# The third pair of the last step of both MLPs takes seven products

## The chip, the cores and the metric

One core of a Trainium2 chip runs the whole program. The metric is the time of one execution on the device, in microseconds. TensorE (PE) multiplies, VectorE (DVE) and ScalarE (ACT) work on elements, GpSimd (POOL) and SyncE (SP) mostly issue transfers here.

## The reference

A decoder trunk of two layers on 256 tokens of width 2048, everything float32. Every sub-layer is `h = h + rmsnorm(f(rmsnorm(h)))`. Layer 0 is a gated convolution and an MLP; then a shared K and V are projected; layer 1 is an attention without softmax and another MLP. The MLP has a hidden width of 8192:

```python
def sq_relu_mlp(u, w_up, w_down):
    return jnp.square(jax.nn.relu(u @ w_up)) @ w_down
```

The change concerns only the down product of the two MLPs, and of it one piece of 256 hidden units by 1024 output columns.

## The kernel before, in words

**Precision.** Each operand of a product is split into a rounded high part and the rest, the low part. A product of two blocks is three matmuls into the same PSUM bank: high by high, high by low, low by high (L1194 to L1196 in `products`, L327 to L329 in `Group.half`). The high parts of weights are written by ScalarE (L174), the low parts by VectorE (L185).

**Weights.** The weights are one stream of chunks of 128 x 1024, in the order in which they are used. SP loads a chunk into one of five `raw` buffers (`load_one`, L158). `split_one` rounds it into one of seven ring buffers `hi` and one of seven `lo`. A raw buffer takes the next load when its chunk is split; a ring buffer is free when PE has used its chunk. `chunk(i)` asks for splits up to four chunks ahead.

**The MLP.** It goes in 8 steps of 1024 hidden units (8 hidden tiles of 128, 4 pairs). In step e, PE alternates between one hidden tile of step e+1 (`whole_up`) and one pair of step e on the way down (`Down.pair`). Down goes by two halves of 1024 columns. The last step has no tile to make any more: in its first half the four pairs follow each other on PE (`for m in range(4): down.pair(...)`), and the second half is a plain `Group` of eight chunks on the banks 6, 7, 0 and 1 (`LAST_BANKS`). In the first MLP its last four chunks are taken block by block (`KeyNorms`, edge 4), in the second its last six (`OutNorms`, edge 6): there the chunks 762 to 767 all go by the first block and the first 512 columns before anything else, so they follow each other within 0.68 us each.

**Eight products or seven.** A pair is two hidden tiles by two token blocks, times two chunks of two column halves of 512: a 2 x 2 block product. `Down.eight` does it plainly with 8 products into four banks. `Down.seven` does it with 7 products, from sums of the blocks (Winograd's form of Strassen's algorithm). It needs sums of the weights, made by `split_seven` (four subtractions of 128 x 512, L211, then seven half-chunks to round and to subtract instead of four, in four ring buffers a, b, t, u instead of two), and sums of the hidden blocks, made by `Hidden.sums_of` (four of 128 x 128, L1056, and their splits, L1012 and L1013). Four of its products, with the keys 1, 5, 6 and 7, are collected over several pairs in banks 6, 7, 0 and 1. They are added crosswise to the results afterwards: during the steps through memory by POOL's transfers (`add_later`), in the last step at once by VectorE (`add_now`: one copy on ScalarE, L1165, and eight adds on VectorE, L1166 to L1172).

**Which pairs take seven.** The table `SEVEN` holds, for each step and half, the pairs with seven products. In the steps 0 to 6 all pairs take seven. In the last step, before the change, only pair 0 of the first half does. A pair with seven in one half alone is `apart`: its hidden tiles are also split plainly, and its first sum gets a tile of its own with the tag "d".

**When the shared products end.** `Down.range` gives the pair at which each bank's collecting begins and ends. The banks of the keys 1, 5, 6 and 7 end at the last pair with seven products; there `add_now` is put into the program. The second half takes these four banks next.

**What sets the order.** PE's order is that of the program. For VectorE and ScalarE a planner lists the instructions by their place in the program and by when it reckons them ready, `tc.high_priority()` ahead of others; each engine then takes its list in order. The sums of the last pair into the results (L1141), their squares (ScalarE) and gains (L503) are of high priority. From the last chunks of the second half on (`begin`), VectorE and ScalarE too follow the program.

Of the kernel before, what the change touches and what calls it, by code (L numbers as in the profile page):

```python
# [10 lines left out]
F32R = mybir.dt.float32r  # L11
# [3 lines left out]
P = 128  # L15
# [31 lines left out]
STEPS = 8  # L47
# [2 lines left out]
DOWN_BANKS = {(0, 0): 3, (0, 1): 4, (1, 0): 5, (1, 1): UP_BANK, 1: 6, 5: 7, 6: 0, 7: 1}  # L50
LAST_BANKS = [[6, 7], [0, 1]]
OUT_SEVENS = (4, 6)
SEVEN = [((0, 1, 2, 3),) * 2] * (STEPS - 1) + [((0,), ())]
ORDER = ((0, 1, 2, 3), (1, 2, 3, 0))

IN_N = [j * KD + i for i in range(KD) for j in range(3)]
# [40 lines left out]
def trunk(ctx, tc, x, xT, vecs, rows, ws, out):  # L97
# [906 lines left out]
    def mlp(pool, i, before, after):  # L1004
# [5 lines left out]
        def two_parts(parts, src):  # L1010
            hi, lo = parts
            nc.scalar.activation(hi, src, AF.Copy)  # L1012
            nc.vector.tensor_tensor(lo, src, hi.bitcast(F32), op=ALU.subtract)  # L1013

        class Hidden:


            def __init__(self, e):
                self.xs, self.sums = [None] * (NF // 4), {}
                first, second = SEVEN[e]  # L1020
                self.pairs = [2 * m for m in first]
# [23 lines left out]
            def sums_of(self, n, both):  # L1045

                t = after.dump()
                s2, s3, s4 = (t[:, j * P : (j + 1) * P] for j in range(3))
                a11, a21, a12, a22 = (both[:, j // 2, j % 2 * P : (j % 2 + 1) * P] for j in range(4))
                apart = n in self.apart  # L1050
                s1 = t[:, 3 * P :] if apart else a21
                for to, v, w, op in (
                    (s3, a11, a21, ALU.subtract), (s1, a21, a22, ALU.add),
                    (s2, s1, a11, ALU.subtract), (s4, a12, s2, ALU.subtract),
                ):
                    nc.vector.tensor_tensor(to, v, w, op=op)  # L1056
                if apart:
                    one = pool.tile([P, 2, P], F32R, tag="d", name="sums", bufs=1)
                    one = [one[:, j, :] for j in range(2)]
                    two_parts(one, s1)  # L1060
                else:
                    one = self.x(n, 1)
                    hi, lo = (self.xs[n // 4][:, n % 4 : n % 4 + 2, j] for j in range(2))
                    two_parts((hi, lo), both[:].rearrange("p k (b t) -> p k b t", b=NB))
                more = pool.tile([P, 6 * P], F32R, tag="hg", name="sums", bufs=5)
                more = [more[:, j * 3 * P : (j + 1) * 3 * P] for j in range(2)]
                two_parts(more, t[:, : 3 * P])
                return [one] + [[m[:, j * P : (j + 1) * P] for m in more] for j in range(3)]
# [105 lines left out]
        class Down:  # L1174


            def __init__(self, j, plan):
                self.j, self.plan, self.ps = j, plan, {}
                sevens_at = [at for at in plan if at[1] in SEVEN[at[0]][at[2]]]
                whole_at = [at for at in plan if at not in sevens_at and at[0] == STEPS - 1]  # L1180
# [17 lines left out]
            def pair(self, at, first, xs):  # L1198
                e, m, _ = at
                seven = m in SEVEN[e][at[2]]  # L1200
                (self.seven if seven else self.eight)(at, first, xs, 2 * m)
# [34 lines left out]
        for e in range(STEPS):  # L1236
            for h in range(2):
                for m in SEVEN[e][h]:
                    n = 16 * h + 4 * ORDER[h].index(m) + 2 if e < STEPS - 1 else 8 * h + 2 * m
# [308 lines left out]
```

## Time and profile before

| | us |
|---|---|
| median of 3 runs | 2097.27 (2096.62 to 2098.21) |
| the profiled execution | 2096.79 |
| its span on the core | 2095.0 |
| TensorE busy | 2079.7 (99%) |
| VectorE busy | 1888.3 (90%) |
| ScalarE busy | 1456.1 (70%) |

One execution was profiled; its page gives shares of the span, and the trace gives each instruction's start and duration in microseconds from the start of the span. The duration of a matmul's row covers its way through the array, and the next one starts before it ends. A row such as `DVE L185 TENSOR_TENSOR wlo<-raw,whi` is an operation of VectorE at line 185 that writes a low part; what stands in brackets is how long the engine was idle before it and what ended that. Chunks with sums carry their number and letter (`whi752a`); plain chunks have none in these rows and are counted.

### The profile page before, as it was taken

The numbers are of one execution on the slowest core, as the hardware profiler recorded it, in microseconds if no ns is written. First come the engines' busy times: TensorE is split into PE (matmuls) and PEld (weight loads), VectorE is DVE, ScalarE is ACT, GpSimd is POOL, SyncE is SP. The second block draws the span as 40 slices with busy tenths as digits, with TensorE's granted clock in tenths as the row PEclk, the third lists the DMA queues.
The fourth block names the chain that finished last, engine by engine and source line by source line (L and its number), as shares of the span: only waits on it lengthen the run. The fifth ranks groups of instructions, "written<-read, shape, count | busy, mean of one in ns | idle before, by whom it ended". The sixth has DMA issues, their size and how long they took to land.

```text
span 2095.0 us, 29733 instructions
## 1 busy us (share of the span) xinstructions
PE 2079.7 (99%) x10566; PEld 1774.8 (85%) x10566; DVE 1888.3 (90%) x2811; ACT 1456.1 (70%) x2132; POOL 112.6 (5%) x137
## 2 busy tenths in 40 slices
PE   9999999999999999999999999999999999999998
PEld 8888888888888888888888888889888888888886
DVE  8999996999999999999766777658999999999997
ACT  8666554776777777777567888547877767677773
POOL 0000000000100101001000000000001010010010
PEclk9999999999999999999999999999999999999999
DMA  8467674677778878779575555665687787787884
GB/s 291 149 204 251 199 248 155 193 231 227 239 221 234 237 217 251 224 230 261 181 220 167 161 161 161 221 181 171 181 256 232 221 241 225 233 245 219 232 241 164
DMA packets 132341, 449.23 MB, mean 214 GB/s; under 512 B 14816, under 2 KB 15072, under 8 KB 131168
## 3 DMA queue, kind: packets, MB, share of 16 engines
q1 hardware_dynamic: 113184, 406.55, 60.9%
q0 software_dynamic: 18720, 40.38, 9.7%
q8 instruction: 83, 1.36, 0.3%
q14 instruction: 66, 0.54, 0.1%
q10 hardware_dynamic: 288, 0.39, 0.1%
HBM read 413.19 MB, written 2.10 MB: 198 GB/s over the span
## 4 chain that ended last, share of the span: by engine, by line
PE 94%; DVE 4%; issue 1%; DMA 1%; ACT 0%; SPq 0%; DVEq 0%; ACTq 0%
PE up L1081 21%; PE up L1088 12%; PE acc L327 7%; PE acc L329 7%; PE acc L328 7%; PE more L1195 5%; PE more L1194 5%; PE more L1196 5%; PE acc L813 5%; PE acc L1194 4%; PE acc L1195 4%; PE acc L1196 4%; DVE wlo L185 1%; PE up L1083 1%; PE tr L264 1%
## 5 line engine op out<-in xcount | busy, mean ns | idle before, releaser
L185 DVE TENSOR_TENSOR wlo<-raw,whi 128x1024 fp32r<-128x1024 f32 (+1 forms) x414 | 495.9, 1207 | 67.6 <-ACT whi L174 67.3
L174 ACT ACTIVATE whi<-raw 128x1024 fp32r<-128x1024 f32 (+1 forms) x414 | 424.7, 1044 | 152.3 <-PE acc L329 63.5
L1081 PE MATMUL up<-u,whi 128*128 128x512 f32 x1952 | 465.0, 389 | 0.0
L1081 PEld LDWEIGHTS up<-u,whi 128*128 128x128 f32 x1952 | 365.0, 188 | 74.7
L1088 PEld LDWEIGHTS up<-u,wlo 128*128 128x128 f32 x2048 | 263.6, 191 | 10.3
L1088 PE MATMUL up<-u,wlo 128*128 128x256 f32 x2048 | 268.1, 283 | 0.0
L211 DVE TENSOR_TENSOR sums<-raw,sums 128x512 f32<-128x512 f32 x260 | 179.3, 690 | 0.9
L187 DVE SCALAR_TENSOR_TENSOR wlo<-raw,gv,whi 128x512 fp32r<-128x512 f32 (+1 forms) x160 | 131.9, 854 | 41.7 <-ACT whi L174 40.9
L174 ACT ACTIVATE whi<-raw,gv 128x512 fp32r<-128x512 f32 (+1 forms) x160 | 121.6, 800 | 48.6 <-PE acc L329 42.2
L327 PE MATMUL acc<-whi,u 128*128 128x512 f32 x384 | 153.1, 399 | 0.1
L329 PE MATMUL acc<-whi,u 128*128 128x512 f32 x384 | 149.9, 390 | 0.0
L328 PE MATMUL acc<-wlo,u 128*128 128x512 f32 x384 | 149.8, 390 | 0.0
L1094 ACT ACTIVATE half<-up 128x256 f32<-128x256 f32 x128 | 49.1, 385 | 129.8 <-PE up L1088 127.2
L1101 POOL DMA_DIRECT2D mg<-more x108 | 94.0, 870 | 825.8 <-ACT more L1156 423.9
L813 PE MATMUL acc<-u,whi 128*128 128x512 f32 x416 | 98.9, 391 | 2.7 <-DVE sum L822 2.7
L211 DVE TENSOR_TENSOR sums<-raw,raw 128x512 f32<-128x512 f32 x130 | 89.8, 691 | 7.2 <-DMA raw<-w_mlp 7.1
L813 PEld LDWEIGHTS acc<-u,whi 128*128 128x128 f32 x416 | 77.4, 188 | 20.5 <-DVE sum L822 3.7
L211 DVE TENSOR_TENSOR sums<-raw 128x512 f32<-128x512 f32 x130 | 89.8, 691 | 2.2 <-DMA raw<-w_mlp 1.6
L329 PEld LDWEIGHTS acc<-whi,u 128*128 128x128 f32 x384 | 72.1, 188 | 15.4
L327 PEld LDWEIGHTS acc<-whi,u 128*128 128x128 f32 x384 | 72.2, 188 | 13.9 <-ACT tk L1380 0.6
L328 PEld LDWEIGHTS acc<-wlo,u 128*128 128x128 f32 x384 | 72.3, 188 | 13.4
L1034 ACT ACTIVATE s<-s 128x256 f32<-128x256 f32 x128 | 52.1, 411 | 12.1 <-DVE s L1033 11.6
(6686 smaller groups left out, 4589.3 us busy)
## 6 DMA issues: line engine op xcount, KB each, us to landing
raw<-w_mlp SPq DMA_DIRECT2D x512, 512.0 KB, 4.6
raw<-w_in SPq DMA_DIRECT2D x94, 512.0 KB, 4.5
mg<-more POOLq DMA_DIRECT2D x108, 256.0 KB, 6.2
raw<-w_out SPq DMA_DIRECT2D x32, 512.0 KB, 4.6
raw<-w_v SPq DMA_DIRECT2D x32, 512.0 KB, 4.5
raw<-w_k SPq DMA_DIRECT2D x32, 512.0 KB, 4.4
raw<-w_q SPq DMA_DIRECT2D x32, 512.0 KB, 4.3
raw<-w_wo SPq DMA_DIRECT2D x32, 512.0 KB, 3.8
```

The lines of the kernel that those rows point to most:

```text
L174: rounded = nc.scalar.activation(hi[:, at], raw[i][:, at], AF.Copy, scale=1.0 if gain is None else gain)
L185: nc.vector.tensor_tensor(lo[:, at], t[:, at], hi[:, at].bitcast(F32), op=ALU.subtract)
L211: nc.vector.tensor_tensor(t, x, y, op=ALU.subtract)
L327: nc.tensor.matmul(ps[:], xh, hi[:, a], start=i == 0 and k == 0, stop=False)
L328: nc.tensor.matmul(ps[:], xh, lo[:, a], start=False, stop=False)
L329: nc.tensor.matmul(ps[:], xl, hi[:, a], start=False, stop=i == self.n - 1 and k == self.ks - 1)
L813: nc.tensor.matmul(ps[:, :cols], w, xs[:, :cols], start=k == 0 and part == parts[0], stop=k == KD - 1 and part == parts[1], skip_group_che ...
L1081: nc.tensor.matmul(ps, weight(0, first, m), x, start=k == 0, stop=False)
L1088: nc.tensor.matmul(pss[n][:, :T], weight(1, first, m), x, start=False, stop=k == KD - 1)
L1194: nc.tensor.matmul(self.ps[key][:], xh, hi, start=first, stop=False)
L1195: nc.tensor.matmul(self.ps[key][:], xh, lo, start=False, stop=False)
L1196: self.done = nc.tensor.matmul(self.ps[key][:], xl, hi, start=False, stop=last)
```

## The change

The third pair (number 2) of the last step is added to the pairs with seven products, in the first half of the columns, in both MLPs. The tag "d" gets a second buffer, since now two pairs of that step are `apart`.

```diff
-SEVEN = [((0, 1, 2, 3),) * 2] * (STEPS - 1) + [((0,), ())]
+SEVEN = [((0, 1, 2, 3),) * 2] * (STEPS - 1) + [((0, 2), ())]
...
                 if apart:
-                    one = pool.tile([P, 2, P], F32R, tag="d", name="sums", bufs=1)
+                    one = pool.tile([P, 2, P], F32R, tag="d", name="sums", bufs=2)
```

What follows from the table: pair 2 goes through `Down.seven`, its two chunks through `split_seven`, its hidden tiles through `sums_of` as well. The keys 1, 5, 6 and 7 are collected until pair 2, so `add_now` comes behind pair 2 rather than behind pair 0, with one pair left before the second half takes their banks. The bank of the eight-product pairs' last block collects pairs 1 and 3 only.

## The prediction

> **What bounds the kernel now.** I read the page first (engine shares, clock, chain that ended last), then the stretches of the last step of the second MLP, then the timelines of TensorE, VectorE and ScalarE there, and the same of the first MLP. First the page:
>
> ```profile
> PE 2079.7 (99%) x10566; PEld 1774.8 (85%) x10566; DVE 1888.3 (90%) x2811; ACT 1456.1 (70%) x2132; POOL 112.6 (5%) x137
> PEclk9999999999999999999999999999999999999999
> PE 94%; DVE 4%; issue 1%; DMA 1%; ACT 0%; SPq 0%; DVEq 0%; ACTq 0%
> ```
>
> TensorE carries 94% of the chain at full clock, so products taken away are time, as long as what feeds them is ready. VectorE, at 90%, is second. The table by stretch cuts the second MLP's last step at its pairs (columns: stretch, its length, then PE, PEld, DVE, ACT, POOL busy with counts, clock, DMA share, GB/s):
>
> ```profile
> 2043.50:2048.30 4.80, 4.80 (x23) 3.96 (x22) 4.80 (x6) 3.66 (x5) 0.87 (x1) 1.00 0.89 218
> 2048.30:2053.70 5.40, 5.40 (x25) 4.49 (x24) 5.40 (x9) 2.59 (x3) 0.55 (x1) 1.00 1.04 376
> 2053.70:2059.20 5.50, 5.50 (x26) 4.54 (x25) 4.07 (x4) 2.07 (x3) 0.00 (x0) 1.00 0.97 357
> 2059.20:2064.60 5.40, 5.40 (x25) 4.47 (x24) 4.82 (x6) 2.74 (x5) 0.00 (x0) 1.00 0.57 222
> 2064.60:2070.00 5.40, 5.40 (x25) 4.50 (x24) 5.20 (x6) 4.69 (x9) 0.00 (x0) 1.00 0.01 2
> ```
>
> Here PE never rests, VectorE is full for 10 us and nearly full later, and ScalarE has room everywhere. So the question is what VectorE's new work does to weight parts that PE will want.
>
> **What goes: products.** Pair starts on PE (start, duration, line, operands):
>
> ```profile
> 2043.52 0.39 PE L1194 MATMUL more<-whi752a,hid 128*128 128x512 f32 x1
> 2048.28 0.39 PE L1194 MATMUL acc<-whi,hid 128*128 128x512 f32 x1
> 2053.72 0.39 PE L1194 MATMUL acc<-whi,hid 128*128 128x512 f32 x1
> 2064.60 0.39 PE L327 MATMUL acc<-whi,hid 128*128 128x512 f32 x1
> 2073.44 0.39 PE L327 MATMUL acc<-whi,hid 128*128 128x512 f32 x1
> ```
>
> Chunks are counted as in the trace's names: the second MLP's last step begins at 752, so the third pair is 756/757, the fourth 758/759, the eight chunks of the second half 760 to 767. The seven-product pair (21 matmuls) takes 2048.28 - 2043.52 = 4.76 us, the eight-product pair (24) 5.44 us; a matmul costs 0.227 us of issue, not the 0.39 of its row, since they overlap. The change takes 3 x 0.227 = **0.68 us** off PE in each MLP, 1.36 in all, and no more: this is the ceiling of the gain.
>
> **What comes: VectorE and ScalarE work.** The first pair's split shows what the third will cost:
>
> ```profile
> 2034.61 0.69 DVE L211 TENSOR_TENSOR sums<-raw 128x512 f32<-128x512 f32 x1
> ...
> 2036.41 0.69 DVE L185 TENSOR_TENSOR wlo752a<-raw,whi752a 128x512 fp32r<-128x512 f32 x1
> 2037.01 0.69 DVE L211 TENSOR_TENSOR sums<-raw,sums 128x512 f32<-128x512 f32 x1
> 2038.04 1.23 DVE L185 TENSOR_TENSOR wlo752b<-raw,whi752b 128x1024 fp32r<-128x1024 f32 x1 [0.34 <-PE up L1088]
> 2039.19 1.22 DVE L185 TENSOR_TENSOR wlo752t<-sums,whi752t 128x1024 fp32r<-128x1024 f32 x1
> ...
> 2042.18 2.51 DVE L185 TENSOR_TENSOR wlo<-raw,whi 128x1024 fp32r<-128x1024 f32 x2 [0.23 <-ACT whi L174]
> 2044.60 0.42 DVE L259 TENSOR_TENSOR hid<-s,hid 128x256 fp32r<-128x256 f32 x1
> 2044.94 1.22 DVE L185 TENSOR_TENSOR wlo<-raw,whi 128x1024 fp32r<-128x1024 f32 x1
> ```
>
> From start to start a 128x512 costs 0.60 us and a 128x1024 1.13. The split of the third pair becomes 4 sums (2.40) + low part a (0.60) + b, t, u (3.39) = 6.39 us in place of 2 x 1.13 = 2.26: **+4.13 us**. The sums of the hidden pair are made once more; the first pair's are these:
>
> ```profile
> 1981.52 0.29 DVE L1056 TENSOR_TENSOR sq<-s 128x128 f32<-128x128 f32 x1
> 1983.40 0.29 DVE L1013 TENSOR_TENSOR sums<-sq,sums 128x128 fp32r<-128x128 f32 x1
> 1985.54 0.56 DVE L1013 TENSOR_TENSOR sums<-sq,sums 128x384 fp32r<-128x384 f32 x1
> ...
> 2024.43 0.42 DVE L259 TENSOR_TENSOR hid<-s,hid 128x256 fp32r<-128x256 f32 x1
> ```
>
> Four small sums and the small split at 0.20 from start to start, the wide split 0.47: **+1.47 us**, from about 2024 on, since the third pair's second hidden tile is split at 2024.43 (the last row). ScalarE gets 3 half-width roundings more (about 0.48 each) and two small ones, some 2 us; its stretches above leave 1 to 3 us free in each, so this I cost at nothing. The second buffer of tag "d" costs no instruction; it only lets the second set of sums exist beside the first. The hg buffers: five, and a sixth set is wanted in step 7, but step 6 is through with its pair 1 three pairs before its end at 2043.52, before 2024: nothing.
>
> **The Trainium skill on this price.** VectorE: DVE Perf Modes, section "The DRAIN you can't avoid", says that the next VectorE operation doesn't start until the pipe is empty. By it operations stand behind each other at their full 0.69 and 1.22 us, the split grows by 4.67 us, the list of 17.15 us reckoned below by about an eighth, and the sum comes to some +2.3 us. The rows start 0.60 and 1.13 apart, so the trace disagrees and its spacing is used.
>
> **What moves: the adding of the shared products.** Keys 1, 5, 6, 7 now end with the third pair, not the first, so add_now (one ScalarE copy, eight VectorE adds, no DMA) runs about 10 us later. Before, and behind it:
>
> ```profile
> 2046.07 0.69 DVE L1172 TENSOR_TENSOR mg<-mg,more 128x512 f32<-128x512 f32 x1
> ...
> 2047.81 0.68 DVE L1166 TENSOR_TENSOR more<-more 128x512 f32<-128x512 f32 x1
> ...
> 2051.94 1.29 DVE L1172 TENSOR_TENSOR mg<-mg,more 128x512 f32<-128x512 f32 x2
> 2053.14 4.63 DVE L185 TENSOR_TENSOR wlo<-raw,whi 128x1024 fp32r<-128x1024 f32 x4
> 2059.77 1.23 DVE L185 TENSOR_TENSOR wlo<-raw,whi 128x1024 fp32r<-128x1024 f32 x1 [2.00 <-ACT whi L174]
> ...
> 2069.00 1.22 DVE L185 TENSOR_TENSOR wlo<-raw,whi 128x1024 fp32r<-128x1024 f32 x1
> 2070.14 0.75 DVE L503 SCALAR_TENSOR_TENSOR mg<-mg,hs,gpost 128x512 f32<-128x512 f32 x1
> ```
>
> Eight adds are 4.8 us. In the new order key 6 ends at 2053.72 + 15 x 0.227 = 2057.1, so the first PSUM add can't start earlier, and 7 of the 8 adds (4.2 us) fall into the stretch after 2057, where so far the low parts of 763 to 767 and the last adds stand. Bank 7 (key 5) must be free for the second product of the second half, 2064.6 after the change. Four adds from 2057.3, even with two low parts between them, end near 2062: 2.6 us to spare, no wait.
>
> **VectorE's clock in the second MLP, after.** It reaches chunk 756 at 2044.94 + 1.47 less the two idle bits quoted (0.34, 0.23) = 2045.8. The third pair is split by 2052.2; PE wants it from 2053.72 on, its last factors about 4 us later: no wait. 758 ends at 2053.4. 759 needs a ring buffer that PE frees at about 2053.0, and a rounding on ScalarE (1.06): low part done 2055.4. 760: 2056.6, one add: 2057.2. What is left before PE can finish: 7 adds (4.2), 761 to 764 (4.52), four adds of sums L1141 (2.4), four gains L503 (0.66 each, 2.64), 765 to 767 (3.39): 17.15 us, to 2074.35 if VectorE never rests. Before, 767's low part ended at 2070.2 against PE's use at 2073.44 (3.2 us of slack), one gain behind it. With one gain behind it again it ends at 2073.7; PE, 0.68 earlier, wants it with its second matmul, 2072.99. **Wait: 0.7 us**; with all gains ahead of it 1.36; with 761 and 762 better placed and the gains late (three behind it) none. I take 1.0, the upper half, since a semaphore and a ScalarE rounding stand between. Second MLP: -0.68 + 1.0 = **+0.3 us**. The wait would be on PE at L328, behind it only the rest of that group; the tail from the last matmul to the end is unchanged.
>
> Transfers and roundings:
>
> ```profile
> 2044.71 1.80 SPq L158 DMA_DIRECT2D raw<-w_mlp  x2
> 2047.92 2.06 SPq L158 DMA_DIRECT2D raw<-w_mlp  x2
> raw<-w_mlp SPq DMA_DIRECT2D x14, 512.0 KB, 5.6
> L174 ACT ACTIVATE whi<-raw 128x1024 fp32r<-128x1024 f32 x406 | 421.9, 1056 | 151.0 <-PE acc L329 63.5 <-PE up L1081 37.1 <-DMA raw<-w_mlp 10.7
> ```
>
> The last row is the rounding of a whole chunk on ScalarE, 1.06 us, used above. Two loads are issued behind the whole split rather than one behind each half, so those of 761 and 762 move from 2046 to 2048 to about 2049 to 2051; with 5.6 us to landing in this stretch they land by 2057, when needed at 2057 to 2063. SP has nothing else; the row load on POOL keeps its place. Nothing, but it is the thinnest cover.
>
> **The first MLP** has the same pairs 1060.5 us earlier, but its second half runs four chunks by both blocks (edge 4, not 6), so 383 is wanted later:
>
> ```profile
> 1004.08 0.39 PE L327 MATMUL acc<-whi,hid 128*128 128x512 f32 x1
> 1008.48 1.23 DVE L185 TENSOR_TENSOR wlo<-raw,whi 128x1024 fp32r<-128x1024 f32 x1
> 1013.62 1.28 DVE L187 SCALAR_TENSOR_TENSOR wlo<-raw,gv,whi 128x1024 fp32r<-128x1024 f32 x1 [1.44 <-ACT whi L174]
> 1017.00 0.39 PE L327 MATMUL acc<-whi,hid 128*128 128x512 f32 x1
> ```
>
> VectorE would end the same list at 2074.35 - 1060.5 = 1013.9, PE wants it at 1016.5: 2.6 us to spare, and VectorE rested 1.44 us there anyway. **-0.68 us.**
>
> Sum: -0.68 + 0.3 = **-0.4 us**. The profiled execution took 2096.79 us (span 2095.0), 0.5 below the median 2097.27. On the median: **2096.9 us**.
>
> **Rivals.** (a) All hidden: the gains come late, VectorE's wait is nought, both MLPs gain 0.68: 2095.9. For it: 3.2 us of slack before. Against: 5.6 us of new work and 4.2 moved into a stretch with 2.0 us of rest.
>
> (b) Slower: the moved adds stand in VectorE's queue ahead of the low parts of 759 to 761. VectorE takes its list in order, so it would rest from 2053.4 to 2057.3 for key 6's bank, add until 2061.5, and give 759 at 2062.6; PE wants its low part at 2058.48 + 0.68 + 0.23 = 2059.4. Wait 3.2 us, in both MLPs; in the second, 767 then ends 3.0 us later than reckoned, 4.3 us behind PE's wish. Sum: (3.2 - 0.68) + (4.3 - 0.68) = +6.1: 2103.4. It decides from 1.9 us of extra rest in each MLP. Against: before, low parts were put between these adds (2046 to 2052) and no add waited. TensorE: Matmul & The Clock Gate, section "Architectural detail", states that ScalarE and VectorE queues are strict first in, first out, which is what this rival needs; the 2.00 us rest at 2059.77 fits it. The same page, "The HAM clock gate", has an idle window of about 3.4 us halve the clock; no row here shows it: the clock row above is nines throughout.
>
> (c) That the products aren't saved can't be: the count of matmuls is fixed by the text.
>
> **How the numbers follow.** My forecast 0.54 (own range 2095.6 to 2098.5: waits of 0 to 2 us in the second MLP, and the runs' spread), (a) 0.25, (b) 0.17, with 0.04 for changes of order elsewhere, half of it each way. 0.2% is 4.2 us, about what a measurement of this kernel can tell from no change. The forecast and (a) lie within it; only (b) leaves it. Faster 0.02, same 0.79, slower 0.19. The range runs from 2095.2 to 2100.0, which holds the forecast, (a) and the mild part of (b).
>
> **What would show it.** 10560 matmuls; third pair 4.76 us in both MLPs; add_now's L1166 near 2057.3 and 996.8; a PE wait at L328 of 0.5 to 1.5 us near 2072 in the second MLP and none near 1016. Wrong if PE waits at the fourth pair or at the start of the second half, or if VectorE shows rests of 2 us or more on L1166.

## The result, and the profile after

| | before | after |
|---|---|---|
| median of 17 runs each, us | 2098.09 (2096.4 to 2100.25) | 2102.26 (2099.69 to 2106.38) |
| the profiled execution, us | 2096.79 | 2101.15 |
| its span, us | 2095.0 | 2099.4 |

The ratio is **1.0022, with a 95% interval of 1.0016 to 1.0029**: 3.4 to 6.1 us slower. (A ratio here is taken over all runs of both kernels, so it can differ a little from the quotient of the two medians.) The forecast of 2096.9 and its range (to 2100.0) were too low.

The page of the kernel after: instruction counts and busy time, and the shares of the chain that ended last.

```profile
PE 2080.0 (99%) x10560; PEld 1772.2 (84%) x10560; DVE 1899.8 (90%) x2835; ACT 1462.2 (70%) x2140; POOL 112.6 (5%) x137
PE 89%; DVE 5%; issue 3%; DMA 1%; ACT 1%; POOL 0%; SPq 0%; DVEq 0%; POOLq 0%; ACTq 0%
```

Six matmuls fewer, 11.5 us more of VectorE, 6.1 of ScalarE; PE's share of the chain falls from 94% to 89%, VectorE's rises from 4% to 5%. Something now waits. To find it I cut both traces at the same PE matmuls: "pairs" runs from the first matmul of the last step's first pair to the first of its second half; "half 1" from there to the first transposition (L264) of the next stage, in the first MLP; "half 2" from there to the last matmul, in the second. All are differences of start times on PE's timeline, in us:

| kernel | pairs 1 | half 1 | pairs 2 | half 2 | sum against before |
|---|---|---|---|---|---|
| before | 21.08 | 19.73 | 21.08 | 21.53 | |
| after | 20.40 | 22.14 | 20.40 | 23.36 | +2.88 |

PE's timeline of the kernel after (start, duration, operation, in brackets the idle time before it), where the waits and most of these starts stand (the first pair of the first MLP started at 984.20):

```profile
1004.60 0.39 PE L327 MATMUL acc<-whi,hid 128*128 128x512 f32 x1
1026.74 0.44 PE L264 MATMUL tr<-ident,h 128*128 128x128 f32 x2 [2.26 <-DVE h L571]
...
2046.80 0.39 PE L1194 MATMUL more<-whi752a,hid 128*128 128x512 f32 x1
2057.00 0.39 PE L1194 MATMUL more<-whi756a,hid 128*128 128x512 f32 x1
2061.76 0.39 PE L1194 MATMUL acc<-whi,hid 128*128 128x512 f32 x1
2067.20 0.39 PE L327 MATMUL acc<-whi,hid 128*128 128x512 f32 x1
...
2075.65 0.50 PE L328 MATMUL acc<-wlo,hid 128*128 128x512 f32 x1 [0.17 <-DVE wlo L185]
...
2077.92 0.50 PE L328 MATMUL acc<-wlo,hid 128*128 128x512 f32 x1 [0.17 <-DVE wlo L185]
2090.56 0.39 PE L329 MATMUL acc<-whi,hid 128*128 128x512 f32 x1
```

The pairs gained exactly 0.68 us in each MLP (the third now takes 2061.76 - 2057.00 = 4.76). Both second halves lost more: **+2.41 us in the first MLP**, in one rest of 2.26 in front of a transposition that waits for the residual L571, and **+1.83 in the second**, in small rests as PE follows VectorE chunk by chunk (1.13 us from chunk to chunk, VectorE's pace, where PE alone takes 0.68).

The second MLP. Its stretches after (columns as before), then VectorE's timeline:

```profile
2057.00:2061.80 4.80, 4.80 (x23) 3.98 (x22) 4.19 (x5) 4.29 (x6) 0.00 (x0) 1.00 0.96 355
2061.80:2067.20 5.40, 5.40 (x25) 4.47 (x24) 5.40 (x9) 2.99 (x5) 0.00 (x0) 1.00 0.83 285
2067.20:2072.60 5.40, 5.40 (x25) 4.50 (x24) 5.38 (x9) 4.75 (x9) 0.00 (x0) 1.00 0.01 3
```

```profile
2057.61 2.36 DVE L185 TENSOR_TENSOR wlo<-raw,whi 128x1024 fp32r<-128x1024 f32 x2 [2.10 <-ACT whi L174]
2061.63 0.68 DVE L1166 TENSOR_TENSOR more<-more 128x512 f32<-128x512 f32 x1
...
2067.62 1.28 DVE L1141 TENSOR_TENSOR mg<-mg,acc 128x512 f32<-128x512 f32 x2
2070.78 0.74 DVE L503 SCALAR_TENSOR_TENSOR mg<-mg,hs,gpost 128x512 f32<-128x512 f32 x1
2071.45 1.22 DVE L185 TENSOR_TENSOR wlo<-raw,whi 128x1024 fp32r<-128x1024 f32 x1
...
2073.25 4.62 DVE L185 TENSOR_TENSOR wlo<-raw,whi 128x1024 fp32r<-128x1024 f32 x4
```

From 2061.8 on VectorE is full. The adds (from L1166), the four sums L1141 and three of the gains L503 stand ahead of the low part of 763 (2071.45); the fourth gain stands ahead of those of 764 to 767, which come in one run at the very end, to 2077.87.

The first MLP, VectorE after, and behind it the same low part and the same sum L1141 in the kernel before:

```profile
1009.30 1.22 DVE L185 TENSOR_TENSOR wlo<-raw,whi 128x1024 fp32r<-128x1024 f32 x1
1011.10 4.63 DVE L185 TENSOR_TENSOR wlo<-raw,whi 128x1024 fp32r<-128x1024 f32 x4
1015.64 1.28 DVE L187 SCALAR_TENSOR_TENSOR wlo<-raw,gv,whi 128x1024 fp32r<-128x1024 f32 x1
1018.51 2.60 DVE L187 SCALAR_TENSOR_TENSOR wlo<-raw,gv,whi 128x1024 fp32r<-128x1024 f32 x2 [1.59 <-ACT whi L174]
1021.02 0.68 DVE L1141 TENSOR_TENSOR mg<-mg,acc 128x512 f32<-128x512 f32 x1
1025.93 0.75 DVE L571 SCALAR_TENSOR_TENSOR h<-mg,rstd,h 128x512 f32<-128x512 f32 x1
```

```profile
999.25 1.23 DVE L185 TENSOR_TENSOR wlo<-raw,whi 128x1024 fp32r<-128x1024 f32 x1 [1.94 <-ACT whi L174]
1017.88 0.69 DVE L1141 TENSOR_TENSOR mg<-mg,acc 128x512 f32<-128x512 f32 x1 [0.25 <-PE acc L329]
```

SP's loads of the next chunks (the V weights, 384 and on), first after, then before; and ScalarE's roundings of two of them after:

```profile
1010.58 0.33 SPq L158 DMA_DIRECT2D raw<-w_v  x1
...
1014.38 1.16 ACT L174 ACTIVATE whi<-raw,gv 128x1024 fp32r<-128x1024 f32 x1 [4.71 <-DMA raw<-w_v]
1017.32 1.15 ACT L174 ACTIVATE whi<-raw,gv 128x1024 fp32r<-128x1024 f32 x1 [1.78 <-DMA raw<-w_v]
```

```profile
1000.50 2.06 SPq L158 DMA_DIRECT2D raw<-w_v  x2
```

These rows make one chain. The low part of chunk 379 stands behind the adds, sums and gains and comes at 1009.30 instead of 999.25. A raw buffer is free only when its chunk is split, so the first load of a V chunk goes out at 1010.58 instead of 1000.50. ScalarE waits for the data (4.71 and 1.78 us), VectorE gives the low parts of 385 and 386 only from 1018.51 on, and L1141 of the second half's first sum stands behind them in its list: 1021.02, where before it waited for nothing but PE and came at 1017.88. The norm and the residual L571 follow, and PE waits 2.26 us.

The kernels of the next section bear the chain out. Counted from the first matmul of the second half, the first load of a V chunk goes out at -3.6 us before, and at 6.0 after, 5.5 in `first_only` and 5.7 in `third_alone`, which have the wait; at 2.1 in `early` and 1.0 in `posts_late`, which don't.

### The profile page after: what moved, and what is told of

Its sections match the earlier page's. It is cut to its first block, busy times and chain, and to the rows that moved or that the text cites. A ratio compares the mean times of both kernels' runs of the same rounds, so it can differ in the third digit from the quotient of the medians.

```text
span 2099.4 us, 29747 instructions
## 1 busy us (share of the span) xinstructions
PE 2080.0 (99%) x10560; PEld 1772.2 (84%) x10560; DVE 1899.8 (90%) x2835; ACT 1462.2 (70%) x2140; POOL 112.6 (5%) x137
## 4 chain that ended last, share of the span: by engine, by line
PE 89%; DVE 5%; issue 3%; DMA 1%; ACT 1%; POOL 0%; SPq 0%; DVEq 0%; POOLq 0%; ACTq 0%
PE up L1081 20%; PE up L1088 11%; PE acc L327 7%; PE acc L329 7%; PE acc L328 7%; PE more L1195 5%; PE more L1194 5%; PE more L1196 5%; PE acc L813 5%; PE acc L1194 4%; PE acc L1195 4%; PE acc L1196 4%; DVE wlo L185 2%; PE up L1083 1%; PE tr L264 1%
## 5 line engine op out<-in xcount | busy, mean ns | idle before, releaser
L185 DVE TENSOR_TENSOR wlo<-raw,whi 128x1024 fp32r<-128x1024 f32 (+1 forms) x410 | 490.0, 1205 | 65.9 <-ACT whi L174 65.3
L187 DVE SCALAR_TENSOR_TENSOR wlo<-raw,gv,whi 128x512 fp32r<-128x512 f32 (+1 forms) x160 | 131.9, 854 | 40.0 <-ACT whi L174 39.2
L327 PE MATMUL acc<-whi,u 128*128 128x512 f32 x384 | 153.1, 399 | 0.1
L328 PE MATMUL acc<-wlo,u 128*128 128x512 f32 x384 | 149.8, 390 | 0.0
L327 PEld LDWEIGHTS acc<-whi,u 128*128 128x128 f32 x384 | 72.2, 188 | 13.8 <-ACT tk L1380 0.6
L328 PEld LDWEIGHTS acc<-wlo,u 128*128 128x128 f32 x384 | 72.3, 188 | 13.4
L813 PEld LDWEIGHTS acc<-u,wlo 128*128 128x128 f32 x416 | 52.8, 191 | 3.6 <-DVE sum L822 2.0
```

What stands on the lines that cost most here:

```text
L185: nc.vector.tensor_tensor(lo[:, at], t[:, at], hi[:, at].bitcast(F32), op=ALU.subtract)
L327: nc.tensor.matmul(ps[:], xh, hi[:, a], start=i == 0 and k == 0, stop=False)
L328: nc.tensor.matmul(ps[:], xh, lo[:, a], start=False, stop=False)
L813: nc.tensor.matmul(ps[:, :cols], w, xs[:, :cols], start=k == 0 and part == parts[0], stop=k == KD - 1 and part == parts[1], skip_group_che ...
```

## Experiments

Two theories stood against my forecast's "none near 1016" and against each other: that the added work of VectorE is too much for what is left of the step, or that the shared products end too late, so that the same adds, sums and gains fall in front of the last low parts.

**One MLP at a time.** `first_only` has the change in the first MLP alone:

```diff
+        last_sevens = ((0, 2), (0,))[i]
+        SEVEN = [((0, 1, 2, 3),) * 2] * (STEPS - 1) + [(last_sevens, ())]
...
-                    one = pool.tile([P, 2, P], F32R, tag="d", name="sums", bufs=1)
+                    one = pool.tile([P, 2, P], F32R, tag="d", name="sums", bufs=2)
```

> The third pair takes seven in the first MLP only; the second is as before. Theory A (the shared products end one pair before the second half, so the eight adds and the gains stand ahead of the low parts of its chunks): the first MLP keeps its share, -0.68 us of products and +2.4 us of a PE wait at the first transposition behind the MLP, together +1.7 us. Theory B (the second buffer of tag d, or run to run spread, and not the order): no difference to the kernel before but -0.7 us.

`second_only` has the two tuples the other way round:

```diff
+        last_sevens = ((0,), (0, 2))[i]
```

> The third pair takes seven in the second MLP only. Theory A: -0.68 us of products and +1.8 us of PE waits for low parts of the last chunks (L328), together +1.15 us, and no PE wait at the first transposition behind the first MLP. Theory B: -0.7 us. With the first MLP's +1.7 this makes 2.9 us of the 4.2 measured; what is missing would have to show in one of the two.

Measured: `first_only` 2100.27 against 2097.85, ratio 1.0011 (1.0002 to 1.0020); `second_only` 2099.68, ratio 1.0010 (1.0001 to 1.0019). PE's waits on VectorE, first of `first_only`, then of `second_only` (total, times, longest):

```profile
PE tr L264 <- DVE h L571: 2.6, 2, 2.3
```

```profile
PEld acc L328 <- DVE wlo L185: 2.4, 4, 0.6
PE tr L264 <- DVE h L571: 0.3, 1, 0.3
```

| kernel | pairs 1 | half 1 | pairs 2 | half 2 | sum against before |
|---|---|---|---|---|---|
| first_only | 20.40 | 22.22 | 21.08 | 21.53 | +1.81 |
| second_only | 21.08 | 19.73 | 20.40 | 23.33 | +1.12 |

The two waits are independent, each with its own MLP, and together they are all that the touched stages lose (1.81 + 1.12 = 2.93; the kernel after has 2.88).

**The late end without the work.** `third_alone` gives seven products to the third pair and eight to the first: as many sums, splits and products as before, and only their end is late.

```diff
-SEVEN = [((0, 1, 2, 3),) * 2] * (STEPS - 1) + [((0,), ())]
+SEVEN = [((0, 1, 2, 3),) * 2] * (STEPS - 1) + [((2,), ())]
```

> The third pair takes seven and the first eight: one pair with seven in the last step as before, the same count of products and of VectorE's work, but the shared products end with the third pair. Theory A (the late adds): both waits come although no work was added; no product is saved, so +2 to +4.5 us. Theory C (the added split and sums, 5.6 us of VectorE in each MLP, are what is too much): no difference, within 0.5 us.

Measured: 2102.18 against 2097.85, ratio 1.0021 (1.0012 to 1.0030). Stages 21.08, **22.37**, 21.08, **23.34**: both waits, +2.64 and +1.81, with no work added. VectorE in the second MLP:

```profile
2061.81 2.36 DVE L185 TENSOR_TENSOR wlo<-raw,whi 128x1024 fp32r<-128x1024 f32 x2 [3.08 <-ACT whi L174]
...
2077.46 4.62 DVE L185 TENSOR_TENSOR wlo<-raw,whi 128x1024 fp32r<-128x1024 f32 x4
```

It even rests 3.08 us before the adds, and the last four low parts still come in one run at the end. So the late end alone is enough to bring both waits; the added work isn't needed for them.

**The work without the late end.** `early` gives seven products to the first and the second pair: the same saving and the same added work as the change, but the shared products end one pair sooner.

```diff
-SEVEN = [((0, 1, 2, 3),) * 2] * (STEPS - 1) + [((0,), ())]
+SEVEN = [((0, 1, 2, 3),) * 2] * (STEPS - 1) + [((0, 1), ())]
...
-                    one = pool.tile([P, 2, P], F32R, tag="d", name="sums", bufs=1)
+                    one = pool.tile([P, 2, P], F32R, tag="d", name="sums", bufs=2)
```

> The second pair takes seven beside the first, not the third: the same work added and the same six matmuls saved, but the shared products end one pair (5.44 us) earlier. Theory A: both waits gone or nearly, -1.4 to -0.3 us. Theory C: as the changed kernel, +3 to +5 us.

> The second pair takes seven beside the first, once more, to narrow the interval of its ratio (0.9994, 0.9985 to 1.0003 in the first run). By the stages of its trace it gains twice 0.68 us and loses nothing: -1.4 us, a ratio of 0.9993. The rival (the gain is spread): a ratio of 1.000.

Measured: 2096.75 against 2097.85, ratio 0.9994 (0.9985 to 1.0003); again (`early_again`, on another chip) 2097.12 against 2098.21, ratio 0.9993 (0.9985 to 1.0002). Stages in both: 20.40, 19.73, 20.40, 21.53, which is the full gain of 1.36 us and no wait. VectorE in the second MLP:

```profile
2052.54 0.68 DVE L1166 TENSOR_TENSOR more<-more 128x512 f32<-128x512 f32 x1
...
2057.34 3.49 DVE L185 TENSOR_TENSOR wlo<-raw,whi 128x1024 fp32r<-128x1024 f32 x3
...
2070.61 2.35 DVE L185 TENSOR_TENSOR wlo<-raw,whi 128x1024 fp32r<-128x1024 f32 x2
```

Against the step's start (2043.85 here, 2046.80 after the change) the adds begin at 8.7 us instead of 14.8, three low parts come in one run ahead of the sums, and two are left for the end, which is at 29.1 us (2072.96) instead of 31.1 (2077.87). So the added work alone brings no wait. This is the best version of the study. Its medians say -1.1 twice, near the stages' 1.36; each interval still reaches just over 1.

**The late end, with sums and gains behind the low parts.** `posts_late` is the kernel after with the last sums of the first half 6.9 us later in the planner's time and, like their gains, not of high priority:

```diff
+POSTS_LATE = 6.9
...
-            with tc.high_priority():
+            with nullcontext() if isinstance(self, (KeyNorms, OutNorms)) and c < 2 else tc.high_priority():
...
-            with tc.high_priority():
+            with nullcontext() if last and j == 0 else tc.high_priority():
...
-                        add(self.j, b, c, self.ps.pop((b, c)), last)
+                        done = self.ps.pop((b, c))
+                        if last:
+                            later(POSTS_LATE, lambda b=b, c=c, done=done: add(self.j, b, c, done, True))
+                        else:
+                            add(self.j, b, c, done)
```

> The changed kernel, but the last sums (L1141 of before) and gains (L503 of before) of the first half of columns are put into the program 6.9 us of planned time later and without high priority, so that in VectorE's list four of the five low parts of the second half that stood behind them come ahead. Work and products are those of the changed kernel. Theory A (in VectorE's list sums and gains stand ahead of low parts that PE, and the raw buffers, wait for): both waits go, -2.4 and -1.8 us against the changed kernel, so -1.4 us (-1.6 to -0.5) against the kernel before. Theory C (VectorE simply has too much work there): the waits move to the posts or stay, +2 us or more against before.

VectorE in the second MLP (lines stand two to four lower here, so L187 is a low part, L1145 a sum, L1173 an add):

```profile
2063.38 0.68 DVE L1173 TENSOR_TENSOR more<-more 128x512 f32<-128x512 f32 x1
...
2065.18 5.76 DVE L187 TENSOR_TENSOR wlo<-raw,whi 128x1024 fp32r<-128x1024 f32 x5
2070.86 0.68 DVE L1145 TENSOR_TENSOR mg<-mg,acc 128x512 f32<-128x512 f32 x1
```

Five low parts now go ahead of the sums, and both waits are gone: stages 20.40, 19.78, 20.40, 21.53. So the adds of the late end alone don't bring the waits; they come when the sums and gains stand ahead of the low parts too. The median doesn't show the gain: 2098.88 against 2098.26, ratio 1.0003 (0.9994 to 1.0012), which spans -1.3 to +2.5 us. The edit has a price behind the last matmul: from the end of its row to the end of the span this kernel takes 9.71 us, the kernel before 8.49 and the kernel after 8.48. The four stages (-1.31) and this (+1.22) add up to -0.1 us.

`early_posts_late` puts both edits together.

> The second pair takes seven beside the first, and the last sums and gains of the first half stand later in VectorE's list as in posts_late. Theory A says that no wait is left in either, so that this adds nothing: stages of 20.40, 19.73, 20.40 and 21.53 us, -1.4 us against before. If posts_late had a cost of its own beside what it saves (its median came out +0.6 us, not -1.4), it shows here as +1 to +2 us against the run of early in the same call.

Measured: 2099.03 against 2098.21, ratio 1.0007 (0.9998 to 1.0016), with `early`'s stages, but with 9.45 us behind the last matmul, where `early` has 8.48. This is the cost of its own that the expectation named as the other outcome. VectorE's timeline shows where it comes from:

```profile
2077.10 0.75 DVE L507 SCALAR_TENSOR_TENSOR mg<-mg,hs,gpost 128x512 f32<-128x512 f32 x1 [0.94 <-ACT sq L719]
...
2086.42 0.69 DVE L1145 TENSOR_TENSOR mg<-mg,acc 128x512 f32<-128x512 f32 x1
```

Sum, square on ScalarE and gain of the first half now follow each other one by one, with a rest of some 0.9 us before each gain, while the results of the second half wait behind them. So the very last sum starts 1.39 us after the last matmul (2085.03); in the kernel before it is 0.43 (2086.56 against 2086.13). In `posts_late` it is 1.66. Stages and end together give -0.4 us. The median lies 1.9 us above that of `early` in the same comparison; 1.0 of it is the longer end, and for the rest the profiled execution (2096.57, the shortest of its runs) has no sign.

**The first MLP's chain cut in its middle.** `two_less_ahead` is the kernel after with 385 and 386 split two chunks later, so that they no longer stand ahead of L1141:

```diff
-            count["limit"] = groups[-1].first + groups[-1].n - 1 + RING - leave.edge
+            count["limit"] = groups[-1].first + groups[-1].n - 1 + RING - leave.edge - 2 * isinstance(leave, KeyNorms)
```

> The changed kernel, but behind the first MLP two chunks of the next weights fewer (385 and 386, the second and third of the V weights) are split ahead of the last results of the MLP, so their low parts no longer stand ahead of the first sum of those results in VectorE's list. Theory A (raw buffers freed late, loads of those chunks late, VectorE waits for them with the sum behind): the wait at the first transposition, 2.4 us in the changed kernel, falls to 0 to 0.5 us; some of it may come back later as a wait for weights. The second MLP keeps its 1.8 us. Rival (the sum itself, or its PE products, are late): the wait stays at 2.4 us.

VectorE in the first MLP, then PE's waits behind it:

```profile
1014.70 1.28 DVE L187 SCALAR_TENSOR_TENSOR wlo<-raw,gv,whi 128x1024 fp32r<-128x1024 f32 x1
1017.92 0.69 DVE L1141 TENSOR_TENSOR mg<-mg,acc 128x512 f32<-128x512 f32 x1 [1.94 <-PE acc L329]
```

```profile
PE acc L328 <- DVE wlo L187: 6.6, 2, 3.8
PE acc L327 <- ACT whi L174: 1.7, 1, 1.7
```

L1141 is back at 1017.92, and half 1 at 19.73: the wait at the transposition did come from the two chunks ahead of the sum. But the stage behind it then waits 8.3 us for those chunks and loses, by my estimate, some 3.5 us more, since the granted clock in the trace is 0.50 for 3.4 and then 6.8 us there (the last section shows such dips). The time is 2110.87, ratio 1.0058 (1.0044 to 1.0071). The cut shows the link; it is no remedy.

**Controls.** `ctl_two_d` is the kernel before with the second buffer of tag "d" alone; `after_again` is the kernel after, unchanged, in the same comparison.

```diff
-                    one = pool.tile([P, 2, P], F32R, tag="d", name="sums", bufs=1)
+                    one = pool.tile([P, 2, P], F32R, tag="d", name="sums", bufs=2)
```

> The kernel before with the second buffer of tag d and nothing else: the same instructions in the same order. Theory A: no difference, within 1 us of before, and the same times by stage in the last steps. Theory B (the buffer, by the addresses that it moves): part of the 4.2 us.

> The changed kernel once more, for a second profiled execution. The first shows +2.9 us in the last steps and behind them, the median +4.2. Theory D (the rest is spread of the stages ahead of the change, which all kernels have): the last steps again -0.68, +2.4, -0.68, +1.8 within 0.2 us each. Theory E (the wait at the first transposition hangs on transfers and differs from one execution to the next): +2.4 there becomes another number, by 0.5 us or more.

Measured: the buffer 2098.42 against 2098.26, ratio 0.9998 (0.9989 to 1.0007), stages as before: it costs nothing. The kernel after again: 2101.54, ratio 1.0019 (1.0011 to 1.0028), with waits of +2.81 and +2.25 in its profiled execution instead of 2.41 and 1.83. In the second MLP ScalarE waited for a load there, and a gain for ScalarE:

```profile
2066.67 1.06 ACT L174 ACTIVATE whi<-raw 128x1024 fp32r<-128x1024 f32 x1 [1.71 <-DMA raw<-w_mlp]
...
2069.76 0.75 DVE L503 SCALAR_TENSOR_TENSOR mg<-mg,hs,gpost 128x512 f32<-128x512 f32 x1 [0.46 <-ACT sq L715]
```

So the size of the waits varies by some 0.4 us between executions, in the second MLP with the time at which a load landed. That is more than theory D allowed and less than theory E asked for. Whether a sixth raw buffer would take the loads out of the chain was not tried.

## Why the prediction was wrong, point by point

- **Products: right.** 10560 matmuls, 0.68 us in each MLP, 4.76 us for the third pair.
- **Price of the split, sums and second buffer: right.** In the second MLP VectorE's list was to end at 2074.35 on the clock of the trace before; it ended at 2077.87 - 3.28 (how much later the step began, 2046.80 against 2043.52) = 2074.6. The forecast set this against the Trainium skill (VectorE: DVE Perf Modes, "The DRAIN you can't avoid") in its strict form, by which each operation waits for an empty pipe. The same section adds that a next operation that isn't held starts earlier, and with this the trace agrees: the four low parts above took 4.62 us, 1.13 from start to start, with rows of 1.22.
- **Place of the adds: nearly.** L1166 was forecast at 2057.3 and came at 2061.63 - 3.28 = 2058.35; no wait at the fourth pair, none for the four banks.
- **Wait in the second MLP: mechanism right, size off.** I forecast rests at L328 because 765 to 767 come last, 1.0 us, or 1.36 with all four gains ahead. All four gains were ahead, and it measured 1.83. Instead of +0.3 the second MLP gave 1.83 - 0.68 = +1.15. The choice between "all gains ahead" and "the gains late" was made by the middle of my bounds, where the text of the kernel decided it: gains and sums are of high priority.
- **First MLP: the step that failed.** "2.6 us to spare" compared the end of VectorE's list with chunk 383 and stopped there. 383 wasn't late (PE has no rest at L328 in the first MLP). The rest of 1.44 us that it quoted as spare time stood in front of an L187, which is already the low part of a V chunk, so its own lines had the next stage's work in VectorE's list. What was late were the buffers that the chunks 379 to 383 free, hence the loads of the next stage, hence the splits that stand in front of L1141. The "Transfers" step called the loads "the thinnest cover", looked at those of 761 and 762 in the second MLP, and never asked for the loads that follow in the first; the second MLP has none, since the stream ends there. In place of -0.68 it gave 2.41 - 0.68 = +1.73.
- **Rival (b)** had the right kind (adds in an in-order list ahead of low parts) and the wrong place. It put the adds ahead of 759 to 761, with a rest of VectorE on L1166 and PE waiting at the fourth pair. There is no such rest: L1166's row has no bracket. The low parts held up were 763 to 767 and 379 to 383. In front of 763 stood six adds (3.6 us), four sums and three gains (4.4 us together); `posts_late` took away the sums and gains alone, and that was enough.
- **Rival (a)**, all hidden, is what `early` shows, with the pair chosen otherwise.

The touched stages give +2.9 us for the kernel after and, with the larger waits, +3.7 for its second profile; the medians give +4.2 and +3.3. The last section says what lies between, as far as the traces show it.

## What to carry to other kernels

When an edit makes something end later, put all the work that hangs on that end (adds, sums, gains, by their priority) into the in-order list of the engine that does it, and see which operand is pushed to the end of the list. Then follow that operand past its own use: the buffer that it frees, the load that waits for the buffer, the next stage's work on that load, and who stands behind that work in the same list. Where several places save the same, take the one whose shared results end first: here the second pair instead of the third turned a ratio of 1.0022 into 0.9994, though the interval of the latter still holds 1. And follow a remedy in the same way: `posts_late` took both waits away and paid 1.2 us for it behind the last matmul, in the list that it had filled.

## What was not expected of the hardware

**A rest of PE of some 2 us is sometimes followed by 3.4 us at half clock.** Stretches of 1 us of `after_again` behind its wait at the transposition (2.66 us there), columns as in the tables above (the third number from the end is the granted clock):

```profile
1028.00:1029.00 1.00, 0.00 (x0) 0.00 (x0) 0.40 (x2) 0.50 (x3) 0.00 (x0) 1.00 0.01 4
1029.00:1030.00 1.00, 0.43 (x2) 0.43 (x3) 1.00 (x2) 0.00 (x0) 0.00 (x0) 0.51 0.00 0
...
1032.00:1033.00 1.00, 1.00 (x5) 0.78 (x5) 0.70 (x2) 1.00 (x2) 0.00 (x0) 0.79 0.00 0
1033.00:1034.00 1.00, 1.00 (x6) 0.82 (x5) 0.35 (x1) 0.07 (x1) 0.00 (x0) 1.00 0.00 0
```

The same in `ctl_two_d`, behind a wait of 1.82 us at L327 far ahead of the change:

```profile
272.00:273.00 1.00, 0.00 (x0) 0.00 (x0) 0.04 (x1) 1.00 (x3) 0.00 (x0) 1.00 0.95 365
275.00:276.00 1.00, 1.00 (x4) 0.81 (x3) 1.00 (x3) 0.82 (x1) 0.00 (x0) 0.50 0.00 0
278.00:279.00 1.00, 1.00 (x6) 0.82 (x5) 1.00 (x3) 0.18 (x1) 0.00 (x0) 1.00 1.01 279
```

And the kernel after, behind the same wait at the transposition (2.26 us), without it:

```profile
1025.00:1026.00 1.00, 0.00 (x0) 0.00 (x0) 0.23 (x2) 0.67 (x3) 0.00 (x0) 1.00 0.00 0
1028.00:1029.00 1.00, 1.00 (x6) 0.82 (x5) 0.93 (x2) 1.00 (x4) 0.00 (x0) 1.00 0.00 0
```

In `after_again` the four slices from 1029 to 1033 lack 0.49, 0.50, 0.50 and 0.21 us of clock, 1.7 in all, which at half clock is 3.4 us. In `third_alone` and `first_only` rests of 2.49 and 2.34 us at the same transposition left the clock at 1.00, so the length alone doesn't decide. A rest far ahead of the change says the same: near 42 us, in eleven of the twelve profiled executions, PE waits 1.75 to 1.98 us for VectorE (L822), and in four of them (`after_again`, `second_only`, `third_alone`, `posts_late`) 3.4 us at half clock follow, in seven not. The Trainium skill (TensorE: Matmul & The Clock Gate, "What's actually happening") has the clock halved after an idle window of about 3.4 us, and the window runs freely. The traces agree in that the same rest is sometimes followed by a dip and sometimes not, and in the length of the dip. They don't agree that a whole window must be idle, nor with the advice of the Trainium skill (the same page, "Why this matters for your kernels") to avoid rests above about 3 us, if it is read to mean that shorter ones are safe: 1.82 us sufficed. My forecast said that no row of before shows a halved clock. It read the page's clock row, in which each digit covers some 52 us; a dip of 3.4 us doesn't show there, and the trace of before has one, with 0.50 from 8 to 10 us.

This accounts for part of what the stages left open. The stage from the first product near 270 us to the pairs of the first MLP has the same code in all these kernels. It took 713.15 us before, 714.33 after, 715.52 in `after_again` and 716.88 in `ctl_two_d`; less its waits at L327 (none, 0.90, 2.07, 1.82) and the dip in `ctl_two_d` (1.7) it is 713.15, 713.43, 713.45 and 713.36. And from the transposition to the pairs of the second MLP `after_again` took 1021.28 us where before took 1019.72: of these 1.6 us some 1.4 are the dip shown above, which began 0.56 us ahead of the transposition. The length of an execution goes with its mean clock as well: of the 27 runs of before beside `after_again`, 10 with a mean of 0.999 average 2097.1 us, 16 with 0.998 average 2098.9, and one with 0.997 took 2102.0; of `after_again` 3, 5 and 3 runs average 2100.5, 2101.5 and 2104.5. At equal clock the change costs 2.6 to 3.4 us, as the stages say. That the rest of the difference in the medians (4.2 us over all runs) is dips that the new rests bring on more often is likely by this count, but the runs are few, and it isn't shown by itself: of the four profiled executions with the long rest at the transposition (after, `after_again`, `first_only`, `third_alone`), one has the dip there.

Two things stay open: why the waits near 42 us and at L327 differ between executions of the same code, and why the median of `early_posts_late` lies 0.9 us further above that of `early` than its longer end explains.
